# A fixed order for the opening loads and for VectorE's first steps in a two-layer mLSTM/Conformer trunk

## The chip, the core and the metric

The kernel runs on one core of one Trainium2 chip. The metric is the device time of one execution in microseconds (us); lower is better. Five engines matter: TensorE (PE; its weight loads are PEld), VectorE (DVE), ScalarE (ACT), GpSimd (POOL) and SyncE (SP), whose queue issues every transfer of this kernel.

## The reference, cut to what matters

Two layers work on x (512 tokens by 1024 features, float32). The opening of the first layer is what the change touches:

```python
c_act = silu(c)
mod = c_act @ w_ada[l] + b_ada[l]            # 1024 x 6144: six groups of 1024: shift, scale, gate, twice
sh_mix, sc_mix, gt_mix, sh_mlp, sc_mlp, gt_mlp = split(mod, 6)
h = rms_norm(x, g_pre_mix[l]) * (1 + sc_mix) + sh_mix
u = h @ w_in[l]                              # 1024 x 4096: mLSTM input, gate z, GLU a, GLU b
```

After it come the mLSTM heads, a causal convolution over 31 taps behind a GLU, an output projection, and a squared-ReLU MLP with 4096 hidden features. Each sub-layer is normalised, gated and added to x.

## The kernel before, in words

Features lie on partitions: x is eight tiles of 128 features by 512 tokens. A float32 product is made of three matmuls on rounded parts: weight-high by input-high, weight-high by input-low, weight-low by input-high (`passes`, lines 179 to 181). So every weight block is loaded as `raw`, rounded to its high part on ScalarE (L171), and the remainder is taken as the low part (L172); every input tile `hp[i]` has a high part (ScalarE, L359) and a low part (VectorE, L360).

The opening of layer 0 runs in this chain:

- x is loaded, squared on ScalarE (L811) and summed over tiles on VectorE (L813). TensorE sums over partitions (L816), VectorE scales (L817), GpSimd takes the power -1/2 (L818), and TensorE spreads the result over partitions into the bank `bc0` (L824).
- The vector c, broadcast as `cbc` and as the column `cc`, goes through silu (L212, L215, L216).
- Shift and scale of feature tiles 0 to 3 come from `ada_col` on VectorE: one multiply-and-sum over a transposed 128x1024 block (`wadt`, L274, 1.28 us each) per column, two columns per tile, and one small addition (L278).
- Shift and scale of tiles 4 and 5, and of 6 and 7, come from `ada_rows(2)` and `ada_rows(3)` on TensorE: four blocks `wadn` each, eight matmuls (L247), a copy on ScalarE (L250), four small matmuls (L252), three small VectorE steps (L260, L258).
- `make_h` forms tile i: s = x times scale times bc0 (VectorE, L353), then L359 and L360.
- Six banks collect the first six blocks of the input projection at once: per tile 18 matmuls (six blocks, three passes) with the block `win0[i]` (128x768). Then the projections of the mixer follow, beginning with `ps_mm<-slot,yt`; and the 31-tap convolution starts on VectorE (L429, L431), in 480 steps of 0.75 us over both layers, mostly beside TensorE's projections.

The program's order on each engine is set by a scheduler that simulates the program while it is built; `high_priority` shifts an instruction's claim, and `behind(later, earlier)` forces an order. Before the change the scheduler is free to choose the order of the loads and of most of VectorE's steps. Buffers: `raw` has four, `adr` (the blocks of `ada_rows(3)` and later) three, `slot` 25; each of SP's transfers takes one of eight semaphores in turn, so that a transfer is issued only when the eighth before it has landed.

Of the kernel before, what the change touches and what calls it, by code (L numbers as in the profile page):

```python
# [53 lines left out]
def trunk(ctx, tc, xT, vecs, bg, cst, ccol, crow, wadn, wadt, win, win0, wqkv, wgate, wout, wff1, wff2, yT):  # L54
# [34 lines left out]
    def slot(shape=(P, 2, T), dt=F32):  # L89
        return slots.tile(list(shape), dt, name="slot", tag="slot", bufs=NSLOT)  # L90
# [23 lines left out]
    def r32(ap):  # L114
        return ap.bitcast(F32R)
# [4 lines left out]
    cbc = slots.tile([P, 2, T], F32, name="cbc", tag="slot", bufs=NSLOT).rearrange("p a b -> p (a b)")  # L120
    x = [keep.tile([P, T], F32, name=f"x{i}") for i in range(NF)]
    cc = keep.tile([P, NF], F32, name="cc")
    sp.dma_start(out=cbc, in_=crow.broadcast_to([P, D]))
    sp.dma_start(out=cc, in_=ccol)
    for i in range(NF):
        sp.dma_start(out=x[i], in_=xT[i])
        if i == 4:
            sp.dma_start(out=cs, in_=cst)
    sp.dma_start(out=vv, in_=vecs)

    ident = cs[:, C_ID:C_ID + P]
    mask = cs[:, C_MASK:C_MASK + P]
# [27 lines left out]
    def wblock(src, alloc=None, lo_eng=None, pri=None):  # L160
        n = src.shape[-1]
        with tc.high_priority(offset=WPRI if pri is None else pri):
            flat = lambda t: t.rearrange("p a b -> p (a b)")
            raw = wpool.tile([P, n], F32, name="raw", tag="raw", bufs=RAW)
            if alloc is not None:
                hi, lo = flat(alloc())[:, 0:n], flat(alloc())[:, 0:n]
            else:
                hi = wpool.tile([P, n], F32, name="whi", tag="whi", bufs=WHI)
                lo = wpool.tile([P, n], F32, name="wlo", tag="wlo", bufs=WLO)
            sp.dma_start(out=raw, in_=src)  # L170
            act.copy(out=r32(hi), in_=raw)  # L171
            wlast[0] = (lo_eng or pool).tensor_tensor(r32(lo), raw, hi, op=ALU.subtract)  # L172
        return hi, lo
# [60 lines left out]
    def ada_rows(nb, tag, alloc=None):  # L234
# [3 lines left out]
        for kk in range(NF // 2):  # L238
            if alloc is not None:
                raw = alloc().rearrange("p a b -> p (a b)")  # L240
            else:
                raw = wpool.tile([P, D], F32, name="adr", tag="adr", bufs=ADR)
            sp.dma_start(out=raw, in_=wadn[nb, kk])
            for j in range(2):
                k = 2 * kk + j
                g = k % 4
                pe.matmul(bk[32 * g:32 * g + 32, :], cc[:, k:k + 1].broadcast_to([P, 32]), raw[:, j * T:(j + 1) * T],  # L247
                          start=(k < 4), stop=(k >= 4), skip_group_check=True)
# [15 lines left out]
    def ada_col(l, c, alloc=None):  # L264
# [4 lines left out]
            raw = alloc().rearrange("p a b -> p (a b)")  # L269
        else:  # L270
            raw = wpool.tile([P, D], F32, name="adr", tag="adr", bufs=ADR)
        sp.dma_start(out=raw, in_=wadt[l, c])
        m, ini = mods[l][:, c:c + 1], inits[l][:, c:c + 1]
        red = dve.tensor_tensor_reduce(raw, raw, cbc, scale, 0.0 if one else ini, ALU.mult, ALU.add, m)  # L274
        if last[0] is not None:
# [1 line left out]
        if one and alloc is not None:  # L277
            dve.tensor_tensor(m, m, ini, op=ALU.add)  # L278
        elif one:
            late.append((l, c))  # L280

    def ada_bias():

# [133 lines left out]
    def mixer(l, hp, pre):  # L417
# [167 lines left out]
                dve.tensor_tensor(gsb, gsb, acc, op=ALU.add)  # L585

        gw = keep.tile([P, 24, 32], F32, name="gw", tag="gw", bufs=1)
        sp.dma_start(out=gw, in_=wgate[l])

        def gates():  # L590
            pi = bank("mm")
# [231 lines left out]
    for c in range(NC):  # L823
        pe.matmul(bc0[:, c * P:(c + 1) * P], r0[:, c:c + 1].broadcast_to([P, P]), ident, start=True, stop=True)  # L824
    hp, pre = [], {}
    for j in range(NF // 2):
        if j > 1:
            ada_rows(j, "ax", slot if j == 2 else None)
        for i in (2 * j, 2 * j + 1):
            if j < 2:  # L830
                ada_col(0, i, slot)
                ada_col(0, 8 + i, slot)
            pre[i] = wblock(win0[i], slot, dve, 0)
            hp.append(slot())
            lasth = make_h(0, i, x[i], bc0, slice(0, T), hp[i], 8, 0)
            behind(lasth, wlast[0])
    sp.dma_start(out=bgt, in_=bg)
    for l in range(L):
        for o, name, f in ((0, "g_cn", 0.5), (8, "b_cn", 0.5), (16, "b_dw", 2.0)):
            behind(dve.tensor_scalar(hgb[:, l, o:o + 8], vec(name, l), f, None, op0=ALU.mult), lasth)  # L840
# [65 lines left out]
```

## Time and profile before

| | |
|---|---|
| runs shown | 1609.22, 1612.67, 1613.26 us; median 1612.67 |
| the profiled execution | 1609.4 us, of which its span is 1607.6 |
| TensorE busy | 1540.3 us (96% of the span), 8020 matmuls |
| VectorE, ScalarE, GpSimd busy | 878.1, 689.8, 799.8 us |
| chain that ended last | TensorE 79% of the span, VectorE 5%, ScalarE and GpSimd 2% each |

The profiled execution lies 1.8 us above its span, and 3.3 us below the median of the runs. Busy time is an average over the whole span; the change lies in the first 75 us.

### The profile page before, as it was taken

The numbers are of one execution on the slowest core, as the hardware profiler recorded it, in microseconds if no ns is written. First come the engines' busy times: TensorE is split into PE (matmuls) and PEld (weight loads), VectorE is DVE, ScalarE is ACT, GpSimd is POOL, SyncE is SP. The second block draws the span as 40 slices with busy tenths as digits, with TensorE's granted clock in tenths as the row PEclk, the third lists the DMA queues.
The fourth block names the chain that finished last, engine by engine and source line by source line (L and its number), as shares of the span: only waits on it lengthen the run. The fifth ranks groups of instructions, "written<-read, shape, count | busy, mean of one in ns | idle before, by whom it ended". The sixth has DMA issues, their size and how long they took to land.

```text
span 1607.6 us, 21227 instructions
## 1 busy us (share of the span) xinstructions
PE 1540.3 (96%) x8020; PEld 1258.6 (78%) x8020; DVE 878.1 (55%) x1761; ACT 689.8 (43%) x1168; POOL 799.8 (50%) x488
## 2 busy tenths in 40 slices
PE   4899998999999999999999999999999999999997
PEld 3676766678998888888899777676799988888887
DVE  6499999752253522347656999997326320012114
ACT  3254663453554322332452666445355432233243
POOL 0176662255744444445871877334674444444462
PEclk9999999999999999999999999999999999999999
DMA  8414333313413555566630222220241233322341
GB/s 327 176 53 140 133 124 106 135 48 105 131 54 111 195 197 178 184 196 233 226 105 8 78 74 79 92 66 27 89 138 62 80 94 101 94 92 92 96 128 53
DMA packets 56270, 188.91 MB, mean 118 GB/s; under 512 B 6376, under 2 KB 8552, under 8 KB 56168
## 3 DMA queue, kind: packets, MB, share of 16 engines
q1 hardware_dynamic: 56168, 187.56, 35.4%
q8 instruction: 63, 1.03, 0.3%
q14 instruction: 39, 0.32, 0.1%
HBM read 185.44 MB, written 2.10 MB: 117 GB/s over the span
## 4 chain that ended last, share of the span: by engine, by line
PE 79%; DVE 5%; ACT 2%; POOL 2%; issue 1%; DMA 0%; ACTq 0%; POOLq 0%; DVEq 0%
PE ps_mm L179 24%; PE ps_mm L180 24%; PE ps_mm L181 24%; PE ps_mm L662 2%; DVE ps_cv L431 2%; PE ps_mm L674 2%; PE ps_ax L318 1%; POOL wlo L172 1%; PE ps_ax L247 1%; ACT whi L171 1%; PE ps_ax L580 1%; PE ps_ax L344 0%; PE ps_ax L649 0%; POOL slot L156 0%; PE ps_ax L703 0%
## 5 line engine op out<-in xcount | busy, mean ns | idle before, releaser
L172 POOL TENSOR_TENSOR wlo<-raw,whi 128x1024 fp32r<-128x1024 f32 (+1 forms) x216 | 499.6, 2314 | 564.5 <-ACT whi L171 555.0
L179 PE MATMUL ps_mm<-slot,whi 128*128 128x512 f32 (+1 forms) x1632 | 623.6, 383 | 6.4 <-ACT slot L155 3.5
L181 PE MATMUL ps_mm<-slot,wlo 128*128 128x512 f32 (+1 forms) x1632 | 621.1, 381 | 5.3 <-POOL wlo L172 4.8
L180 PE MATMUL ps_mm<-slot,whi 128*128 128x512 f32 (+1 forms) x1632 | 622.3, 381 | 0.7 <-POOL slot L156 0.6
L171 ACT CAST whi<-raw 128x1024 fp32r<-128x1024 f32 (+1 forms) x216 | 216.7, 1003 | 497.2 <-PE ps_mm L180 362.8
L179 PEld LDWEIGHTS ps_mm<-slot,whi 128*128 128x128 f32 x1632 | 307.7, 189 | 76.4 <-issue 5.0
L181 PEld LDWEIGHTS ps_mm<-slot,wlo 128*128 128x128 f32 x1632 | 307.9, 189 | 73.6 <-POOL wlo L172 6.3
L180 PEld LDWEIGHTS ps_mm<-slot,whi 128*128 128x128 f32 x1632 | 308.0, 189 | 67.5 <-issue 4.7
L431 DVE SCALAR_TENSOR_TENSOR ps_cv<-slot,vv,ps_cv 128x512 f32<-128x512 f32 x480 | 333.3, 751 | 1.5
L769 DVE TENSOR_TENSOR ps_mm<-rl,ps_mm 128x512 f32<-128x512 f32 (+1 forms) x78 | 46.8, 600 | 284.6 <-ACT rl L768 284.5
L179 PE MATMUL ps_mm<-slot 128*128 128x256 f32 (+1 forms) x568 | 159.9, 295 | 17.9 <-ACT slot L359 11.0
L180 PE MATMUL ps_mm<-slot 128*128 128x256 f32 (+1 forms) x568 | 164.2, 292 | 0.1
L181 PE MATMUL ps_mm<-slot 128*128 128x256 f32 (+1 forms) x568 | 163.0, 290 | 0.0
L179 PEld LDWEIGHTS ps_mm<-slot 128*128 128x128 f32 x568 | 106.9, 193 | 22.7 <-ACT slot L359 13.7
L180 PEld LDWEIGHTS ps_mm<-slot 128*128 128x128 f32 x568 | 109.4, 193 | 2.7 <-issue 0.8
L181 PEld LDWEIGHTS ps_mm<-slot 128*128 128x128 f32 x568 | 109.3, 193 | 1.3
L172 POOL TENSOR_TENSOR slot<-raw,slot 128x1024 fp32r<-128x1024 f32 x34 | 85.2, 2524 | 14.4 <-issue 12.8
L274 DVE CUSTOM_DVE_ANT_0 adr<-adr,cbc,ini 128x1024 f32<-128x1024 f32 x40 | 66.4, 1671 | 23.3 <-DMA adr<-in_wadt 23.3
L147 POOL TENSOR_TENSOR small<-small,mhalf 128x4 f32<-128x4 f32 (+1 forms) x38 | 34.6, 910 | 84.6 <-DVE small L146 79.8
L771 DVE TENSOR_TENSOR slot<-ps_mm,slot 128x512 fp32r<-128x512 f32 (+1 forms) x78 | 46.4, 595 | 37.3 <-ACT slot L770 37.1
L532 POOL TENSOR_TENSOR xa<-xa,s 128x512 f32<-128x512 f32 x48 | 62.0, 1291 | 4.8 <-ACT s L531 1.6
L770 ACT CAST slot<-ps_mm 128x512 fp32r<-128x512 f32 (+1 forms) x78 | 39.9, 511 | 45.8 <-DVE ps_mm L769 45.8
(200 smaller groups left out, 1571.3 us busy)
## 6 DMA issues: line engine op xcount, KB each, us to landing
raw<-in_wff SPq DMA_DIRECT2D x138, 512.0 KB, 3.5
raw<-in_win SPq DMA_DIRECT2D x58, 512.0 KB, 3.3
adr<-in_wadt SPq DMA_DIRECT2D x56, 512.0 KB, 4.5
raw<-in_wout SPq DMA_DIRECT2D x36, 512.0 KB, 3.5
adr<-in_wadn SPq DMA_DIRECT2D x28, 512.0 KB, 4.4
raw<-in_wqkv SPq DMA_DIRECT2D x24, 256.0 KB, 2.6
slot<-in_wadt SPq DMA_DIRECT2D x8, 512.0 KB, 6.0
raw<-in_win SPq DMA_DIRECT2D x8, 384.0 KB, 7.4
```

Of the source, the lines that this page charges most:

```text
L147: pool.tensor_tensor(y, u, mhalf[:, 0:n], op=ALU.pow)
L171: act.copy(out=r32(hi), in_=raw)
L172: wlast[0] = (lo_eng or pool).tensor_tensor(r32(lo), raw, hi, op=ALU.subtract)
L179: pe.matmul(out, whi, xh, start=first, stop=False)
L180: pe.matmul(out, whi, xl, start=False, stop=False)
L181: mark[0] = pe.matmul(out, wlo, xh, start=False, stop=last)
L274: red = dve.tensor_tensor_reduce(raw, raw, cbc, scale, 0.0 if one else ini, ALU.mult, ALU.add, m)
L431: dve.scalar_tensor_tensor(acc, at[i][:, k:k + T], w, acc, op0=ALU.mult, op1=ALU.add)
L532: pool.tensor_tensor(acc, acc, tk, op=ALU.add)
L769: dve.tensor_tensor(o, rl[:, ts], o, op=ALU.mult)
L770: act.copy(out=r32(pr[:, 0, ts]), in_=o)
L771: last[0] = dve.tensor_tensor(r32(pr[:, 1, ts]), o, pr[:, 0, ts], op=ALU.subtract)
```

## The change

All loads of the opening go through `load`, and each is forced behind the one before it; all VectorE steps of the first tiles go through `step`, likewise. The loop over tiles is written out in that order: x first, then `cbc`, `vv`, `cc`; per tile the two `wadt` blocks around `win0`; `ada_rows(2)` stands after tile 1 and `ada_rows(3)` after tile 3 (before: after tile 3 and after tile 5 in the program text); for tiles 0 to 2 the next tile's `ada_col` steps stand around this tile's low parts. The loads of `gw` (gate weights) and `bgt` are put behind the opening's last load.

```diff
     for i in range(NF):
-        sp.dma_start(out=x[i], in_=xT[i])
-        if i == 4:
-            sp.dma_start(out=cs, in_=cst)
-    sp.dma_start(out=vv, in_=vecs)
+        load(x[i], xT[i])
+        if i == 3:
+            load(cs, cst)
+    load(cbc, crow.broadcast_to([P, D]))
+    load(vv, vecs)
+    load(cc, ccol)
...
-        sp.dma_start(out=gw, in_=wgate[l])
+        g = sp.dma_start(out=gw, in_=wgate[l])
+        if l == 0:
+            behind(g, queue[0])
...
-    for j in range(NF // 2):
-        if j > 1:
-            ada_rows(j, "ax", slot if j == 2 else None)
-        for i in (2 * j, 2 * j + 1):
-            if j < 2:
-                ada_col(0, i, slot)
-                ada_col(0, 8 + i, slot)
-            pre[i] = wblock(win0[i], slot, dve, 0)
-            hp.append(slot())
-            lasth = make_h(0, i, x[i], bc0, slice(0, T), hp[i], 8, 0)
-            behind(lasth, wlast[0])
-    sp.dma_start(out=bgt, in_=bg)
+    SPLIT = 4
+    step(laststat)
+    for c in (0, 8):
+        step(ada_col(0, c, slot))
+    for i in range(NF):
...
+        load(raw, win0[i])
+        act.copy(out=r32(hi), in_=raw)
+        pre[i] = hi, lo
+        pr, t, sh = slot(), s2(), mods[0][:, i:i + 1]
+        hp.append(pr)
+        step(dve.scalar_tensor_tensor(t, x[i], mods[0][:, 8 + i:9 + i], bc0, op0=ALU.mult, op1=ALU.mult))
+        act.activation(out=r32(pr[:, 0, :]), in_=t, func=AF.Identity, bias=sh)
+        if i + 1 < SPLIT:
+            step(ada_col(0, i + 1, slot))
+            lasth = step(dve.scalar_tensor_tensor(r32(pr[:, 1, :]), t, sh, pr[:, 0, :], op0=ALU.add, op1=ALU.subtract))
+            step(dve.tensor_tensor(r32(lo), raw, hi, op=ALU.subtract))
+            step(ada_col(0, 9 + i, slot))
+        else:
+            step(dve.tensor_tensor(r32(lo), raw, hi, op=ALU.subtract))
+            lasth = step(dve.scalar_tensor_tensor(r32(pr[:, 1, :]), t, sh, pr[:, 0, :], op0=ALU.add, op1=ALU.subtract))
+        if i in (1, 3):
+            ada_rows(2 + i // 2, "ax", slot if i == 1 else None)
+    behind(sp.dma_start(out=bgt, in_=bg), queue[0])
+    ordered[0] = False
```

Three places where instructions moved. First SP's queue right after x, `cs`, `cbc`, `cc` and `vv`. Here `in_wadt` feeds `ada_col`, `in_wadn` feeds `ada_rows`, and `in_win0` is a tile's weight block. Before:

```order
L272 DMA slot_156<-in_wadt 128x1024
L272 DMA slot_159<-in_wadt 128x1024
L243 DMA adr_277<-in_wadn 128x1024
L243 DMA adr_281<-in_wadn 128x1024
L243 DMA adr_285<-in_wadn 128x1024
L837 DMA bgt_75<-in_bg 4x4
L588 DMA gw_338<-in_wgate 128x768
L170 DMA raw_163<-in_win0 128x768
L170 DMA raw_181<-in_win0 128x768
L170 DMA raw_199<-in_win0 128x768
L170 DMA raw_217<-in_win0 128x768
L272 DMA slot_174<-in_wadt 128x1024
```

After, from the same place:

```order
L127 DMA slot_156<-in_wadt 128x1024
L127 DMA slot_159<-in_wadt 128x1024
L127 DMA raw_165<-in_win0 128x768
L127 DMA slot_172<-in_wadt 128x1024
L127 DMA slot_177<-in_wadt 128x1024
L127 DMA raw_183<-in_win0 128x768
L127 DMA slot_190<-in_wadt 128x1024
L127 DMA slot_195<-in_wadt 128x1024
L127 DMA slot_200<-in_wadn 128x1024
L127 DMA slot_204<-in_wadn 128x1024
L127 DMA slot_208<-in_wadn 128x1024
L127 DMA slot_212<-in_wadn 128x1024
```

Three blocks of `ada_rows(3)` and `gw` have left the place ahead of the first `win0`, and the four blocks of `ada_rows(2)` have come up to before the third. A little later in SP's queue after the change:

```order
L127 DMA raw_245<-in_win0 128x768
L127 DMA adr_255<-in_wadn 128x1024
L127 DMA adr_259<-in_wadn 128x1024
L127 DMA adr_263<-in_wadn 128x1024
L127 DMA adr_267<-in_wadn 128x1024
L127 DMA raw_282<-in_win0 128x768
L127 DMA raw_293<-in_win0 128x768
L127 DMA raw_304<-in_win0 128x768
L127 DMA raw_315<-in_win0 128x768
L871 DMA bgt_75<-in_bg 4x4
L607 DMA gw_338<-in_wgate 128x768
L127 DMA adr_880<-in_wadn 128x1024
```

The four last blocks `win0` now stand behind the fourth block of `ada_rows(3)`, which needs a buffer of the three `adr` and so waits for TensorE's matmuls on the first.

Second, VectorE's queue at tiles 0 and 1 (`cbc` marks `ada_col`, `s2` is the product s, the `slot` with `raw` a weight's low part). Before:

```order
L353 SCALAR_TENSOR_TENSOR s2_170<-x0_77,mod0_101,ps_ax_151 128x512
L172 TENSOR_TENSOR slot_165<-raw_163,slot_164 128x768
L360 SCALAR_TENSOR_TENSOR slot_169<-s2_170,mod0_101,slot_169 128x512
L172 TENSOR_TENSOR slot_183<-raw_181,slot_182 128x768
L274 ISA slot_174,mod0_101<-slot_174,cbc_76,ini0_103 128x1024
L274 ISA mod0_101 128x1
L274 ISA slot_177,mod0_101<-slot_177,cbc_76,vv_74 128x1024
L274 ISA mod0_101 128x1
L278 TENSOR_TENSOR mod0_101<-mod0_101,ini0_103 128x1
L353 SCALAR_TENSOR_TENSOR s2_188<-x1_78,mod0_101,ps_ax_151 128x512
L360 SCALAR_TENSOR_TENSOR slot_187<-s2_188,mod0_101,slot_187 128x512
L172 TENSOR_TENSOR slot_201<-raw_199,slot_200 128x768
```

After:

```order
L859 SCALAR_TENSOR_TENSOR s2_169<-x0_77,mod0_101,ps_ax_151 128x512
L292 ISA slot_172,mod0_101<-slot_172,cbc_76,ini0_103 128x1024
L292 ISA mod0_101 128x1
L863 SCALAR_TENSOR_TENSOR slot_168<-s2_169,mod0_101,slot_168 128x512
L864 TENSOR_TENSOR slot_164<-raw_165,slot_163 128x768
L292 ISA slot_177,mod0_101<-slot_177,cbc_76,vv_74 128x1024
L292 ISA mod0_101 128x1
L296 TENSOR_TENSOR mod0_101<-mod0_101,ini0_103 128x1
L859 SCALAR_TENSOR_TENSOR s2_187<-x1_78,mod0_101,ps_ax_151 128x512
L292 ISA slot_190,mod0_101<-slot_190,cbc_76,ini0_103 128x1024
L292 ISA mod0_101 128x1
L863 SCALAR_TENSOR_TENSOR slot_186<-s2_187,mod0_101,slot_186 128x512
```

One `ada_col` of the next tile has come between a tile's product s and its low part, and the weight's low part now belongs to the tile itself, not to the next one.

Third, TensorE's queue around `ada_rows(2)` (`ps_ax<-slot,cc` are its matmuls). Before it stands behind tile 3:

```order
L181 MATMUL ps_cx<-slot 128x512
L247 MATMUL ps_ax<-slot,cc 32x512 x8
L252 MATMUL ps_ax<-cs,s_245 128x1 x4
L247 MATMUL ps_ax<-adr,cc 32x512 x6
L179 MATMUL ps_mm<-slot 128x512 x3
```

After it stands behind tile 1, and the matmuls of `ada_rows(3)` (`ps_ax<-adr,cc`) follow in two pairs around tile 3's first pass and four behind tile 3:

```order
L199 MATMUL ps_cx<-slot 128x512
L265 MATMUL ps_ax<-slot,cc 32x512 x8
L270 MATMUL ps_ax<-cs,s_216 128x1 x4
L197 MATMUL ps_mm<-slot 128x512 x3
L197 MATMUL ps_cv<-slot 128x512 x2
```

The two `ada_rows` no longer stand together ahead of tile 4. From the end of tile 7 on, every engine's queue holds the same instructions as before with local exchanges of neighbours; the largest are some of the convolution's transposes on TensorE, 13 to 52 matmuls earlier among the projections of layer 0.

## Rows read from the trace of the kernel before

**Rows 1.** Busy time by stretch: stretch in us, its length, then busy us (and instructions) of PE, PEld, DVE, ACT and POOL, the granted clock of TensorE, the busy share of the DMA engines (over 1 is full), GB/s.

```profile
0.00:21.66 21.66, 3.94 (x16) 3.56 (x17) 10.65 (x23) 10.15 (x16) 2.29 (x6) 1.00 0.93 354
21.66:75.30 53.64, 44.61 (x193) 32.02 (x194) 30.28 (x58) 15.67 (x22) 7.39 (x8) 0.97 0.64 234
```

**Rows 2.** Waits of TensorE before 75.3 us: who waited for whom, us in total, times, longest.

```profile
PE ps_mm L179 <- ACT slot L359: 10.5, 6, 2.6
```

**Rows 3.** Transfers of the opening. A line that begins with a time is an issue on SP's queue (start us, us of issuing); the line under it is that transfer alone: KB, and us from issue to landing. The last line but one is from the page: a smaller weight load, median over the span. The last line is the traffic from 8 to 27 us.

```profile
1.65 0.42 SPq L126 DMA_DIRECT2D x<-in_xT  x1
x<-in_xT SPq DMA_DIRECT2D x1, 256.0 KB, 3.6
...
5.43 0.45 SPq L126 DMA_DIRECT2D x<-in_xT  x1
x<-in_xT SPq DMA_DIRECT2D x1, 256.0 KB, 5.3
...
11.75 0.33 SPq L170 DMA_DIRECT2D raw<-in_win  x1
raw<-in_win SPq DMA_DIRECT2D x1, 384.0 KB, 8.4
...
raw<-in_wqkv SPq DMA_DIRECT2D x24, 256.0 KB, 2.6
...
DMA packets 2620, 7.73 MB, mean 407 GB/s; under 512 B 299, under 2 KB 307, under 8 KB 2620
```

**Rows 4.** Timeline of the chain to the first tile: start us, us, engine, line, operation, and in brackets the idle time before and what ended it.

```profile
9.43 2.03 ACT L811 ACTIVATE s<-x 128x512 f32<-128x512 f32 x3 [0.80 <-DMA x<-in_xT]
12.43 1.87 PE L816 MATMUL ps_ax<-cs,rl 128*128 128x1 f32 x8 [12.43 <-DVE rl L813]
13.54 1.23 DVE L216 SCALAR_TENSOR_TENSOR cbc<-raw,cbc 128x1024 f32<-128x1024 f32 x1 [0.70 <-ACT cbc L215]
14.68 0.15 DVE L817 TENSOR_SCALAR small<-ps_ax 128x4 f32<-128x4 f32 x1
...
17.02 2.08 PE L824 MATMUL ps_ax<-cs,small 128*128 128x128 f32 x8 [2.72 <-POOL small L818]
...
19.13 0.75 DVE L353 SCALAR_TENSOR_TENSOR s<-x,mod,ps_ax 128x512 f32<-128x512 f32 x1 [1.65 <-DMA gw<-in_wgate]
20.15 0.83 ACT L171 CAST slot<-raw 128x768 fp32r<-128x768 f32 x1 [6.31 <-DMA raw<-in_win]
20.89 0.72 ACT L359 ACTIVATE slot<-s,mod 128x512 fp32r<-128x512 f32 x1
```

**Rows 5.** Timeline of VectorE at tile 1.

```profile
24.36 1.28 DVE L274 CUSTOM_DVE_ANT_0 slot<-slot,cbc,ini 128x1024 f32<-128x1024 f32 x1 [0.86 <-DMA slot<-in_wadt]
...
28.69 0.75 DVE L360 SCALAR_TENSOR_TENSOR slot<-s,mod,slot 128x512 fp32r<-128x512 f32 x1 [0.79 <-ACT slot L359]
...
29.42 0.96 DVE L172 TENSOR_TENSOR slot<-raw,slot 128x768 fp32r<-128x768 f32 x1
```

**Rows 6.** Timeline of TensorE: first matmuls of tile 0, its last one, first matmuls of tiles 1, 2, 3, 4, 6 and 7, and the first matmul after the opening.

```profile
21.66 1.65 PE L179 MATMUL ps_mm<-slot 128*128 128x512 f32 x3 [2.57 <-ACT slot L359]
...
27.09 0.39 PE L181 MATMUL ps_cx<-slot 128*128 128x512 f32 x1
28.71 0.97 PE L179 MATMUL ps_mm<-slot 128*128 128x512 f32 x3 [1.23 <-ACT slot L359]
...
34.57 0.96 PE L179 MATMUL ps_mm<-slot 128*128 128x512 f32 x3 [1.42 <-ACT slot L359]
...
40.43 0.96 PE L179 MATMUL ps_mm<-slot 128*128 128x512 f32 x3 [1.39 <-ACT slot L359]
...
52.56 0.97 PE L179 MATMUL ps_mm<-slot 128*128 128x512 f32 x3 [1.74 <-ACT slot L359]
...
65.27 1.34 PE L179 MATMUL ps_mm<-slot 128*128 128x512 f32 x3 [2.12 <-ACT slot L359]
...
71.10 0.85 PE L179 MATMUL ps_mm<-slot 128*128 128x512 f32 x3
...
75.28 0.39 PE L179 MATMUL ps_mm<-slot,yt 128*128 128x512 f32 x1
```

**Rows 7.** Timeline of `ada_rows(2)` on TensorE and ScalarE; the fourth pair of matmuls of `ada_rows(3)`; and the load of that pair's block, alone on the queue (KB, us from issue to landing).

```profile
44.80 1.92 PE L247 MATMUL ps_ax<-slot,cc 128*32 128x512 f32 x16
46.79 0.59 ACT L250 COPY s<-ps_ax 128x512 f32<-128x512 f32 x1 [5.68 <-PE ps_ax L247]
47.42 1.05 PE L252 MATMUL ps_ax<-cs,s 128*128 128x1 f32 x8 [0.70 <-ACT s L250]
...
57.41 1.05 PE L247 MATMUL ps_ax<-adr,cc 128*32 128x512 f32 x4
...
adr<-in_wadn SPq DMA_DIRECT2D x1, 512.0 KB, 3.3
```

**Rows 8.** Busy time by stretch as in rows 1: from the last matmul of tile 5 to tile 6, and tile 6's first ten matmuls.

```profile
62.20:65.20 3.00, 0.95 (x9) 0.86 (x7) 1.79 (x5) 0.71 (x2) 0.71 (x6) 1.00 0.77 266
65.27:69.00 3.73, 3.73 (x10) 2.92 (x11) 3.23 (x15) 1.30 (x2) 0.00 (x0) 0.55 0.33 83
```

**Rows 9.** Timeline at one of the convolution's transposes in layer 0: VectorE's last step for it, and TensorE's transposes that read it.

```profile
182.01 1.36 DVE L492 TENSOR_SCALAR csb<-ps_cx,small 128x128 f32<-128x128 f32 x4
...
186.84 0.60 PE L496 MATMUL ps_cx<-cs,csb 128*128 128x128 f32 x4
```

More of the change, by code (lines that the diff above doesn't have):

```diff
@@ L122, in trunk, with load, step @@
     cc = keep.tile([P, NF], F32, name="cc")
-    sp.dma_start(out=cbc, in_=crow.broadcast_to([P, D]))
-    sp.dma_start(out=cc, in_=ccol)
-    for i in range(NF):
-        sp.dma_start(out=x[i], in_=xT[i])
-        if i == 4:
-            sp.dma_start(out=cs, in_=cst)
-    sp.dma_start(out=vv, in_=vecs)
+    queue, steps, ordered = [None], [None], [True]
+    def load(out, in_):
+        d = sp.dma_start(out=out, in_=in_)
+        if ordered[0]:
+            if queue[0] is not None:
+                behind(d, queue[0])
+            queue[0] = d
+        return d
+    def step(inst):
+        if ordered[0]:
+            if steps[0] is not None:
+                behind(inst, steps[0])
+            steps[0] = inst
+        return inst
+    for i in range(NF):
+        load(x[i], xT[i])
[4 more added lines that the diff above has]
+    load(cc, ccol)
     ident = cs[:, C_ID:C_ID + P]
@@ L169, in wblock @@
                 lo = wpool.tile([P, n], F32, name="wlo", tag="wlo", bufs=WLO)
-            sp.dma_start(out=raw, in_=src)
+            load(raw, src)
             act.copy(out=r32(hi), in_=raw)
@@ L242, in ada_rows @@
                 raw = wpool.tile([P, D], F32, name="adr", tag="adr", bufs=ADR)
-            sp.dma_start(out=raw, in_=wadn[nb, kk])
+            load(raw, wadn[nb, kk])
             for j in range(2):
@@ L271, in ada_col @@
             raw = wpool.tile([P, D], F32, name="adr", tag="adr", bufs=ADR)
-        sp.dma_start(out=raw, in_=wadt[l, c])
+        load(raw, wadt[l, c])
         m, ini = mods[l][:, c:c + 1], inits[l][:, c:c + 1]
@@ L280, in ada_col @@
             late.append((l, c))
+        return red
     def ada_bias():
@@ L825, in trunk @@
     hp, pre = [], {}
-    for j in range(NF // 2):
-        if j > 1:
-            ada_rows(j, "ax", slot if j == 2 else None)
-        for i in (2 * j, 2 * j + 1):
-            if j < 2:
-                ada_col(0, i, slot)
-                ada_col(0, 8 + i, slot)
-            pre[i] = wblock(win0[i], slot, dve, 0)
-            hp.append(slot())
-            lasth = make_h(0, i, x[i], bc0, slice(0, T), hp[i], 8, 0)
-            behind(lasth, wlast[0])
-    sp.dma_start(out=bgt, in_=bg)
+    SPLIT = 4
[3 more added lines that the diff above has]
+    for i in range(NF):
+        hi, lo = slot().rearrange("p a b -> p (a b)")[:, 0:6 * P], slot().rearrange("p a b -> p (a b)")[:, 0:6 * P]
+        raw = wpool.tile([P, 6 * P], F32, name="raw", tag="raw", bufs=RAW)
+        load(raw, win0[i])
[17 more added lines that the diff above has]
+    ordered[0] = False
     for l in range(L):
```

## The prediction

> **What bounds the kernel now.** The overview says TensorE is busy for 96% of the span and leads the chain that ended last for 79% of it. So I looked for the stretches where TensorE does not work, with the table by stretch first [rows 1]: it is busy for 3.9 of the first 21.66 us, and 44.6 of the next 53.64, and the end of a matmul is modelled, so busy is not work done. The waits [rows 2] then say what it waits for: ScalarE's high part of an input tile (L359), 10.5 us in six waits. To see what those 53.6 us hold, I read the first matmul of each tile [rows 6]. Tile 7 runs without a gap: 71.10 to 75.28, 4.18 us for its 18 matmuls. At that price seven tiles cost 29.26 us; tile 0, with its slow first matmuls, costs 5.66 (21.66 to 27.09, and 0.23 for the last). Together 34.92 us, so 18.7 us of the stretch are something else: 1.39 before tile 1, 1.68 before each of tiles 2 and 3, 7.95 between tiles 3 and 4 (`ada_rows`), 4.35 between the starts of tiles 4 and 6 beyond two tiles' work, and 1.65 in tile 6 at a slower clock.
>
> The start itself is a chain of single steps [rows 4]: ScalarE squares x as it lands, VectorE sums, TensorE sums over partitions (12.43), VectorE scales (14.68, late because the silu step of `cbc` at 13.54 stands ahead of it and ends at 14.77), GpSimd, TensorE (17.02 to 19.10), VectorE's product s (19.13). Then ScalarE sits in L171 until 20.15, because the first `win0` has only just landed: issued at 11.75, 8.4 us to landing [rows 3]. L359 is queued behind that L171, and TensorE behind L359. All transfers share one pipe, full at 407 GB/s from 8 to 27 us [rows 3], so 512 KB cost 1.29 us of it, 384 KB 0.97.
>
> After 75.28 us nothing is tied to a point in time: weights are loaded and split ahead, and VectorE's convolution starts from the opening's results as TensorE's projections do. What the opening loses or saves goes to the end one to one, unless the local exchanges behind it cost something.
>
> **The change, step by step.**
>
> *x to the head of the queue.* x's first tile was issued at 1.65 behind `cbc` and `cc`; now it takes the place at 0.74 that `cbc` had, 0.91 earlier, and 512 KB (1.3 us of pipe) leave its way. First to last tile took 5.48 us (landings 5.25 and 10.73) [rows 3], and that is kept. The first tile's own latency is not shown for an empty queue: at least 2.6 us, the profile's median for 256 KB transfers later, at most the 3.6 of the row [rows 3]. So x7 lands between 8.8 and 9.8; I take 9.1, nearer the lower end, since nothing is ahead. Squares then end 0.7 later, at 9.8 instead of 11.46: 1.7 us earlier (bounds 1.0 to 2.0). L817 no longer stands behind the silu step: another 0.35. So TensorE's bank `bc0` is done at 17.05 instead of 19.10. The other branch keeps up: `cbc` lands 1.3 behind x7 at 10.4, two ScalarE steps of about 1 end at 12.5, and on VectorE, from 12.85 behind L817, the silu step (1.23) and two `ada_col` (1.28 each) with small steps [rows 4, 5] come to some 4: 16.85.
>
> *First `win0` behind two `wadt` blocks.* From x7's landing 2.4 MB of loads lead to it, 5.9 us: landed at 15.0, cast before s is there. L359 follows s at once: s 17.1 to 17.85, high part 17.9 to 18.6, and TensorE starts at 18.65 instead of 21.66 [rows 4, 6]. **Start: -3.0 us.**
>
> *VectorE's order at tiles 0 to 2.* Per tile it has two `ada_col` steps of 1.28, s 0.75, the weight's low part 0.96 and the input's 0.75 [rows 4, 5]: 5.0 us, above the 4.18 of a tile on TensorE, and that costs the gaps of 1.39 and 1.68. Now one `ada_col` fits into ScalarE's time for L359. Stepping through: tile 0's low parts are there at 20.8, s of tile 1 at 23.1, its high part at 23.9. TensorE leaves tile 0 at 18.65 + 5.66 = 24.3. So the 1.39 before tile 1 is gone, and tile 1 ends at 28.5, its low parts (24.85, 25.8) being in time.
>
> *`ada_rows(2)` ahead of tile 2.* Its four blocks are some 7.0 MB behind x7: landed at 26.2, before TensorE is there. Eight matmuls 2.0 us, copy 0.6, four matmuls 1.05 [rows 7]: 28.6 to 32.25. ScalarE has the copy, a weight cast and L359 in a row, so tile 2 can begin at 32.7. VectorE waits for this too: its three small steps stand ahead of the next `ada_col` and of tile 2's low part, which comes at 34.95, 0.85 after TensorE has done the first six matmuls. Tile 2 ends at 37.75: 4.2 and 0.85 us lost.
>
> *`ada_rows(3)` around tile 3.* A pair of its matmuls costs 1.0 with what lies around it (57.41 to 58.39) [rows 7]. First pair to 38.8; tile 3's high part at 38.95 (VectorE did `ada_col`, the addition and s from 35.75 to 38.2); six matmuls, second pair, twelve matmuls: 44.15. Lost: 1.25 and 1.0. Then four matmuls, the copy (45.9), L359, tile 4 at 47.0: 2.85 lost. SP is held meanwhile: the fourth `adr` block is issued only when the first pair is done, 38.9, and four `win0`, `gw` and the next loads are queued behind it. At 3.3 us alone [rows 7] it is there at 42.2, 2 us before TensorE asks; the next `win0` lands at some 43.3 and is cast by 44.2, 1.1 us before the copy behind it on ScalarE. So I cost this at nothing, with a cover of 1 to 2 us.
>
> *Tiles 4 to 7* have no `ada_col`: VectorE needs 2.5 us per tile, TensorE 4.18. 47.0 + 4 x 4.18 = 63.7 for the first matmul after the opening, against 75.28. Lost in all 10.15 instead of 18.7: **-8.55 us**. The weights of the projection that follows are issued by 52, cast after tile 7's L359 (some 53 us) and split on GpSimd by 59: in time for 63.7.
>
> **Sum.** -3.0 - 8.55 = -11.55: 1609.4 - 11.5 = 1597.9 for the profiled execution. It lies 3.3 below the median of the runs shown and 1.7 below the mean of those three and itself (1611.1); by that mean I forecast **1600 us**.
>
> *The clock, a rule weighed.* In tile 6 the granted clock is 0.55 (the 1.2 GHz level), after 3 us with only 0.95 busy; after the 1.74 us of waiting before tile 4 it was not lowered [rows 6, 8]. The lowered stretch cost 1.65 us. The Trainium skill's page "TensorE: Matmul & The Clock Gate", section "HAM oscillation — how this bites in real kernels", says that TensorE's clock is halved again whenever it waits too long between groups of matmuls, and that every such wait costs anew. The trace agrees for tile 6. By that rule both `ada_rows` would be followed by a slow stretch, since now each is a pause of its own; by the rows of tile 4, neither. The sum above goes by the rows; the rule is the second rival.
>
> **The rivals.**
>
> 1. *The held queue.* The cover of the fourth `adr` block and the `win0` behind it is 1 to 2 us by my sum, whose steps each may be 0.3 off. If the `win0` comes 3 us later than I say, tile 4 starts 2 us later: -9.5, 1601.5 us. For it: nothing else can be issued while SP waits. Against: the pipe is empty by then.
> 2. *A lowered clock after each `ada_rows`*: two stretches at 1.65 us each, none before: -8.2, 1603 us. For it: TensorE has only four tiny matmuls for about 2.1 us before tile 2, and 1.7 before tile 4. Against: tile 4 before, as said.
> 3. *The transposes of the convolution in layer 0*, some 13 to 52 matmuls (3 to 12 us) earlier among the projections. TensorE works in order: a transpose that stands ahead of VectorE's result holds all projections behind it. The slack was 3.5 us at one of them (183.4 to 186.8 [rows 9]); moved by 26 matmuls, 6 us, it could wait 2.5. Four moved ones together are moved by some 26 us. If VectorE's results also shift less than TensorE's work, this eats 3 to 9 of the gain: 1603 to 1609, no change from some 6.8 on. It decides against the change when more than 11.5 + 4.8 = 16.3 of those 26 us are waited for, which gives over 1616 us: slower. Against: VectorE's convolution is moved up with the opening, and the slack was left in most places.
> 4. *No such gain, because something later absorbs it*: a wait on a transfer would. The pipe is far from full after the opening, so I give it little: within 4.8, 1611 us.
>
> **How the numbers follow.** 0.3% is 4.8 us, about what a measurement of this kernel can tell from no change. Chances: the forecast 0.58 (its own range 1596 to 1603: start bounds -1.0 to +0.7, steps 0.3 each, the level of the runs 1.7 either way); rival 1 0.10; rival 2 0.10; rival 3 eating some of the gain 0.13, of which 0.06 still faster by over 4.8; rival 3 turned slower 0.04; rival 4 0.05. Faster 0.58 + 0.10 + 0.10 + 0.06 = 0.84; slower 0.04; within 0.3% 0.12. The range for 8 in 10 goes from 1595, the forecast with every bound on the good side, to 1607, which takes in rivals 1 and 2 and half of 3.
>
> **What would show it.** Right: the first matmul of tile 0 near 18.7, no gap before tile 1, the first matmul after the opening (`ps_mm<-slot,yt`) near 63.7, the same matmul count from there to the end in the same 1532 us. Wrong start: x's squares end near 11 instead of 9.8, or ScalarE still waits for `win0`. Wrong middle: TensorE waits for a block of `ada_rows(3)`, or ScalarE for a `win0` (L855 after the change), before tile 4; or the granted clock near tile 2 or 4 is about half. Wrong end: waits of TensorE on the transposes (L500, L515 after the change) between 110 and 310 us where there were hardly any.

## The result, and the profile after

The changed kernel takes 1596.85 us in the median of four executions (1595.56 to 1600.35); the one before, with a fourth execution beside the three shown, 1612.31. The ratio is 0.9911, 95% interval 0.9889 to 0.9933: faster by 15.5 us, where 0.3% is 4.8. The forecast was 1600, from 1595 to 1607.

The profiled execution of the changed kernel took 1600.35 us, with a span of 1598.6 and a mean granted clock of 0.986 (before 1607.6 and 0.990). So the two traces differ by 9 us, the medians by 15.5; that gap comes up again below. Of the twelve executions of one run below (only the order of VectorE's steps) one took 2551 us, at a mean granted clock of 0.557, and the numbers given there leave it out.

Busy time by stretch, columns as in [rows 1]: up to the first matmul of tile 0, and from there to the first matmul behind the opening.

```profile
0.00:19.78 19.78, 3.94 (x16) 3.56 (x16) 10.93 (x23) 10.34 (x16) 2.17 (x6) 1.00 0.90 338
19.78:67.36 47.58, 45.66 (x193) 32.44 (x194) 29.76 (x59) 16.14 (x22) 7.41 (x8) 0.96 0.75 280
```

The same 193 matmuls that took 53.64 us now take 47.58, and they begin 1.88 earlier: the opening ends at 67.36 instead of 75.28, **7.92 us earlier where 11.55 was forecast**. TensorE's waits in it, all there are:

```profile
PE ps_ax L837 <- DVE rl L834: 12.0, 1, 12.0
PE ps_ax L845 <- POOL small L839: 2.3, 1, 2.3
PE ps_mm L197 <- ACT slot L860: 1.9, 2, 1.6
PE ps_ax L270 <- ACT s L268: 1.5, 2, 0.8
```

The six waits on ScalarE's high part, 10.5 us [rows 2], have become two of 1.9 (L860 is the old L359). The start, as the timelines of ScalarE, TensorE and VectorE have it:

```profile
8.18 2.71 ACT L832 ACTIVATE s<-x 128x512 f32<-128x512 f32 x4 [0.58 <-DMA x<-in_xT]
11.98 1.87 PE L837 MATMUL ps_ax<-cs,rl 128*128 128x1 f32 x8 [11.98 <-DVE rl L834]
13.88 0.16 DVE L838 TENSOR_SCALAR small<-ps_ax 128x4 f32<-128x4 f32 x1 [0.67 <-PE ps_ax L837]
16.11 2.07 PE L845 MATMUL ps_ax<-cs,small 128*128 128x128 f32 x8 [2.27 <-POOL small L839]
16.25 0.83 ACT L855 CAST slot<-raw 128x768 fp32r<-128x768 f32 x1 [2.29 <-DMA raw<-in_win]
18.23 0.75 DVE L859 SCALAR_TENSOR_TENSOR s<-x,mod,ps_ax 128x512 f32<-128x512 f32 x1 [0.32 <-DMA slot<-in_wadt]
19.01 0.72 ACT L860 ACTIVATE slot<-s,mod 128x512 fp32r<-128x512 f32 x1 [1.93 <-DVE s L859]
```

The squares end at 10.89 (before 11.46 [rows 4]), the weight's cast (L855) is over before s begins, and L838 follows L837 at once. Then TensorE: tile 0's first matmul and its last, tile 1's first and last, `ada_rows(2)`, tile 2, the pairs of `ada_rows(3)` around tile 3, tile 4, tile 5's first, and the first matmul behind the opening (compare [rows 6, 7]).

```profile
19.78 0.79 PE L197 MATMUL ps_mm<-slot 128*128 128x512 f32 x1 [1.59 <-ACT slot L860]
26.62 0.40 PE L199 MATMUL ps_cx<-slot 128*128 128x512 f32 x1
26.86 0.62 PE L197 MATMUL ps_mm<-slot 128*128 128x512 f32 x2
30.77 0.39 PE L199 MATMUL ps_cx<-slot 128*128 128x512 f32 x1
31.09 1.92 PE L265 MATMUL ps_ax<-slot,cc 128*32 128x512 f32 x16
33.75 1.05 PE L270 MATMUL ps_ax<-cs,s 128*128 128x1 f32 x8 [0.73 <-ACT s L268]
35.10 0.51 PE L197 MATMUL ps_mm<-slot 128*128 128x512 f32 x1 [0.30 <-ACT slot L860]
41.29 1.05 PE L265 MATMUL ps_ax<-adr,cc 128*32 128x512 f32 x4
42.27 0.96 PE L197 MATMUL ps_mm<-slot 128*128 128x512 f32 x3
47.81 1.06 PE L265 MATMUL ps_ax<-adr,cc 128*32 128x512 f32 x8
50.58 0.71 PE L197 MATMUL ps_mm<-slot 128*128 128x512 f32 x2
54.81 0.39 PE L197 MATMUL ps_mm<-slot 128*128 128x512 f32 x1
67.36 0.39 PE L197 MATMUL ps_mm<-slot,yt 128*128 128x512 f32 x1
```

Tile 0 takes 7.08 us to tile 1's first matmul, tile 1 4.23, tile 2 6.19, tiles 4 to 7 together 16.78. Tile 2's stretch has the granted clock at 0.72, a mean over stretches at the 2.4 and the 1.2 GHz level; in tile 4's it is 1.00:

```profile
35.10:41.29 6.19, 6.09 (x19) 4.12 (x19) 6.08 (x12) 1.40 (x2) 0.00 (x0) 0.72 0.02 4
50.58:54.81 4.23, 4.23 (x20) 3.46 (x20) 4.23 (x9) 2.47 (x5) 0.00 (x0) 1.00 1.02 414
```

Between `ada_rows(3)`'s last matmuls and tile 4, ScalarE shows what the held queue cost: its cast of the next `win0` begins at 46.72 when that block has landed, and then ScalarE waits 1.47 us for TensorE.

```profile
46.72 0.84 ACT L855 CAST slot<-raw 128x768 fp32r<-128x768 f32 x1 [5.71 <-DMA raw<-in_win]
49.03 0.59 ACT L268 COPY s<-ps_ax 128x512 f32<-128x512 f32 x1 [1.47 <-PE ps_ax L265]
```

### The profile page after: what moved, and what is told of

The parts are those of the page before. It is cut to its first block, busy times and chain, and to the rows that moved or that the text cites. A ratio compares the mean times of both kernels' runs of the same rounds, so it can differ in the third digit from the quotient of the medians.

```text
span 1598.6 us, 21226 instructions
## 1 busy us (share of the span) xinstructions
PE 1541.6 (96%) x8020; PEld 1258.7 (79%) x8020; DVE 876.3 (55%) x1761; ACT 690.3 (43%) x1168; POOL 799.3 (50%) x488
## 4 chain that ended last, share of the span: by engine, by line
PE 78%; DVE 3%; ACT 2%; POOL 1%; issue 0%; DMA 0%; POOLq 0%; ACTq 0%
PE ps_mm L197 23%; PE ps_mm L199 23%; PE ps_mm L198 23%; PE ps_mm L695 2%; PE ps_mm L683 2%; PE ps_ax L337 1%; POOL wlo L190 1%; ACT whi L189 1%; PE ps_ax L265 1%; PE ps_ax L670 0%; PE ps_ax L599 0%; PE ps_ax L363 0%; DVE ps_cv L450 0%; PE ps_ax L724 0%; PE ps_cx L500 0%
## 5 line engine op out<-in xcount | busy, mean ns | idle before, releaser
L198 PE MATMUL ps_mm<-slot 128*128 128x256 f32 (+1 forms) x568 | 163.3, 292 | 0.2
L190 POOL TENSOR_TENSOR slot<-raw,slot 128x1024 fp32r<-128x1024 f32 x34 | 86.4, 2563 | 12.8 <-issue 11.2
```

The costliest lines, as they stand in the source:

```text
L198: pe.matmul(out, whi, xl, start=False, stop=False)
```

## The experiments

Twelve further runs were made, in three groups; each group was timed beside the kernel before on its chip (1610.35, 1611.09 and 1610.53 us in the median).

### Again: the changed kernel unaltered

> The changed kernel once more, unaltered. Its first trace has the first matmul after the opening at 67.4 us (75.3 before), 3.7 us later than forecast, and 1531.2 us from there to the end (1532.3 before): 9.0 us less span, while the medians of the runs differ by 15.5 us. Theory: the opening itself varies between executions (x's landings, and how long TensorE stays at its lower clock in tiles 0 and 2), so this trace ends the opening somewhere between 63.7 and 67.4 us with the same 1531 us behind it. Rival: the opening ends at 67.4 us again, and it is the 1531 us behind it that vary by several us from run to run, so that part of the 15.5 us is chance.

Measured: 1595.05 us (1593.28 to 1600.79), ratio 0.9911, interval 0.9894 to 0.9928. Its trace has tile 0 at 19.75 and the end of the opening at 66.81. Both the gain and the shape of the opening repeat. Behind the opening this trace has 1532.2 us, so it does not decide between the theory and its rival.

### Only the new order of the transfers

```diff
     def step(inst):
-        if ordered[0]:
-            if steps[0] is not None:
-                behind(inst, steps[0])
-            steps[0] = inst
         return inst
```

> The changed kernel without the fixed order of VectorE's steps; the loads keep theirs. VectorE now does both low parts of a tile before the next tile's first ada_col. Theory: TensorE then waits again before tiles 1 and 2, about 1 us each, as before the change (1.39 and 1.68 us), so the opening ends some 2 to 3 us later than with the change, about 70 us; time about 2.5 us above the changed kernel. Rival (the order of VectorE's steps is worth nothing, the loads do it all): the opening ends within 1 us of the changed kernel's.

Measured: 1599.94 us (1595.17 to 1602.48), ratio 0.9929, interval 0.9911 to 0.9946; the opening ends at 68.34. VectorE, left to the scheduler, makes a tile's low parts and then the next two `ada_col` steps, and TensorE waits no more for that than in the changed kernel: the end of the opening is 1.0 us later, as the rival says. The time, though, lies 4.9 us above that of the changed kernel beside it (1595.05; 2.8 us by the mean spans), more than the opening shows, and where the rest is lost is not known. Of the whole gain some 10 us come with the transfers and with where `ada_rows` stands.

### Only the order of VectorE's steps

```diff
     def load(out, in_):
         d = sp.dma_start(out=out, in_=in_)
         if ordered[0]:
-            if queue[0] is not None:
-                behind(d, queue[0])
             queue[0] = d
         return d
```

> The changed kernel without the forced order of the loads beyond the first twelve; VectorE's steps keep theirs. Three blocks of ada_rows(3) and then four win0 stand ahead of tile 1's ada_col blocks. Theory: 1.5 MB more ahead of the first win0 makes it land 3.9 us later, so TensorE starts tile 0 near 21.7 us instead of 19.8, and tile 1's ada_col blocks land near 25 us, so tile 1 starts near 28.7 instead of 26.9; the opening ends 3 to 5 us later than with the change. Rival (VectorE's order is what matters): within 1 us of the changed kernel.

Measured: 1606.66 us (1604.8 to 1610.72), ratio 0.998, interval 0.997 to 0.999: 3.7 us of gain. The opening ends at 71.94, 4.6 us later than in the changed kernel, as the theory says; tile 1 begins at 30.79, later than its 28.7. The time lies 11.6 us above the changed kernel's, and for the 7 us of it that are not in the opening no cause is shown. Without its order SP issues three `adr` blocks and four `win0` ahead of tile 1's `wadt`, and VectorE's fixed order, in which tile 0's low part stands behind the next `ada_col`, hangs on that `wadt`. The timeline of TensorE shows where: tile 0 at 21.44, then a wait on the input's low part (L861) inside tile 0 and another inside tile 1.

```profile
21.44 1.65 PE L195 MATMUL ps_mm<-slot 128*128 128x512 f32 x3 [3.52 <-ACT slot L858]
26.12 1.65 PE L196 MATMUL ps_mm<-slot 128*128 128x512 f32 x3 [1.75 <-DVE slot L861]
34.17 0.98 PE L196 MATMUL ps_mm<-slot 128*128 128x512 f32 x3 [1.82 <-DVE slot L861]
```

Here the fixed order on VectorE is worth no more than the order of its inputs lets it be.

### Only x at the head of the queue, in the kernel before

```diff
-    sp.dma_start(out=cbc, in_=crow.broadcast_to([P, D]))
-    sp.dma_start(out=cc, in_=ccol)
...
     for i in range(NF):
-        sp.dma_start(out=x[i], in_=xT[i])
-        if i == 4:
-            sp.dma_start(out=cs, in_=cst)
-    sp.dma_start(out=vv, in_=vecs)
+        load(x[i], xT[i])
+        if i == 3:
+            load(cs, cst)
+    load(cbc, crow.broadcast_to([P, D]))
+    load(vv, vecs)
+    load(cc, ccol)
```

> The kernel before with only the first twelve loads in the new order: x and cs, then cbc, vv, cc. Theory: the first win0 has the same bytes ahead of it as before and still lands near 20 us, and tile 0's high part is queued behind its cast, so TensorE starts tile 0 at 21 to 21.7 us and nothing else moves: time 0 to 1 us below the kernel before. Rival (x at the head is the gain): tile 0 starts 2 us earlier, time 2 us below.

Measured: 1611.15 us (1607.79 to 1615.36), ratio 1.0001, interval 0.999 to 1.0012: nothing. The timeline of TensorE: start, tile 0, and the first matmul behind the opening:

```profile
12.07 1.87 PE L824 MATMUL ps_ax<-cs,rl 128*128 128x1 f32 x8 [12.07 <-DVE rl L821]
16.21 2.07 PE L832 MATMUL ps_ax<-cs,small 128*128 128x128 f32 x8 [2.27 <-POOL small L826]
22.49 1.65 PE L187 MATMUL ps_mm<-slot 128*128 128x512 f32 x3 [4.21 <-ACT slot L367]
...
77.36 0.39 PE L187 MATMUL ps_mm<-slot,yt 128*128 128x512 f32 x1
```

The statistics are as early as in the changed kernel (16.21 against 16.11), and the 0.8 us won there are lost with interest in front of tile 0, in 4.21 us of waiting for ScalarE, 1.6 more than before [rows 6]: ScalarE casts the first `win0` at 20.98, where it did at 20.15 [rows 4]. So tile 0 starts 0.8 us later than before (expected was no later than 21.7), and in this trace the opening ends 2.1 us later; the time does not show them. Moving x forward alone did not pay here; in the changed kernel, where the first `win0` and its two `wadt` come forward with it, tile 0 starts at 19.78.

### `ada_rows(2)` and `(3)` back behind tiles 3 and 5

```diff
-        if i in (1, 3):
-            ada_rows(2 + i // 2, "ax", slot if i == 1 else None)
+        if i in (3, 5):
+            ada_rows(1 + i // 2, "ax", slot if i == 3 else None)
```

> The changed kernel with ada_rows(2) and ada_rows(3) moved back to behind tiles 3 and 5, where they stood before, all else as changed. Theory: each ada_rows costs TensorE about the same pause wherever it stands, and what the change gained is the start and the gaps before tiles 1 to 3: the first matmul behind the opening at 66 to 70 us, the time within 3 us of the changed kernel's. Rival: the gain of the middle is that the pauses were moved to where ScalarE and VectorE need the time anyway: the opening is 5 us or more longer, 72 us or later, and the time 5 us or more longer than the changed kernel's.

Measured: 1604.81 us (1602.6 to 1609.66), ratio 0.9963, interval 0.9951 to 0.9975; the opening ends at 71.00. That is 9 us above the changed kernel's 1595 to 1597 on other chips, 3.6 to 4.2 of them in the opening; for the others, behind it, no cause is shown. The rival holds in the sum (5 us or more), though its 72 us at the end of the opening was 1 too many: a pause of `ada_rows` is cheaper behind tiles 1 and 3. The last pair then has its pause before tile 6, with the lowered clock that stood there before as well (0.66 from 60 to 65 us).

### Where the gain lies: both kernels cut off behind the opening, and behind the mixer

```diff
         at[0], at[1], at[2] = glu_start(3)
+        do_xm(0)
+        ada_rows(4, "ax")
+        (write those tiles as the output)
+        return
```

> The kernel before, cut off behind the opening: it ends after the eight tiles, the first two sixteenths' projections of the mixer and the first ada_rows behind them, and writes tiles made there as the output. Everything later of both layers is left out, so its time stands only beside that of opening_after, the same cut of the changed kernel. Two theories of where the 15 to 16 us between the medians of the full kernels lie, of which the two traces show 7.9 us in the opening (75.28 against 67.36 us at the first matmul behind it) and 1 us behind it. A: the traces show the opening as it is in every execution, and the rest of the gain lies behind it: the two cuts differ by 7 to 9 us. B: the profiled executions of the changed kernel lost clock in the opening that other executions did not lose, and nearly the whole gain is made there: the cuts differ by 11 to 15 us. Between 9 and 11 it stays open.

> The changed kernel, cut off at the same place as opening_before (everything behind the opening and the first two projections is left out). A: 7 to 9 us less than opening_before. B: 11 to 15 us less. In its trace the first matmul of tile 0 is expected at 19.8 and the first matmul behind the tiles at 66.8 to 67.4, as in the two traces of the full kernel.

Measured: 94.03 us (91.22 to 96.89) and 86.24 us (84.31 to 86.67): 7.8 us, theory A; the shortest of each differ by 6.9. But these cuts are not the opening of the full kernels. From tile 6 on TensorE's queue is another: the matmuls of the next `ada_rows` stand among the last tiles, in the cut of the kernel before in the pause ahead of tile 6, and tile 6 then runs at full pace (66.71 to 70.92, 4.21 us). In the second cut the first matmul behind the tiles comes at 69.61, not at 66.8 to 67.4. So the cuts speak against B, but they do not show that other executions of the full kernels have the opening of the traces. In five of the six executions of the second the mean clock was near 0.972, in one 0.990, and that one is the shortest, 84.31: this fits a lowered clock at tile 2 in most of them.

```diff
         hp, pre = mixer(l, hp, pre)
-        hp, pre = mlp(l, hp, pre)
+        for i in range(NF):
+            sp.dma_start(out=yT[i], in_=hp[i][:, 0, :])
+        break
```

> The kernel before, cut off behind the mixer of layer 0: it ends when the input tiles of that layer's MLP are made, and writes these as the output. The MLP of layer 0 and all of layer 1 are left out, so its time stands only beside that of mixer_after, the same cut of the changed kernel. The cuts behind the opening differ by 7.8 us, the full kernels by 15 to 16 us between their medians; where does the rest lie? A: in the convolution of layer 0, which begins from the opening's results and whose steps stand in another order now: the two cuts differ by 12 to 15 us. B: behind the mixer, or nowhere in particular (stretches of lowered clock that fall differently on the two kernels): the cuts differ by 6 to 9 us. The traces of the full kernels show 5.8 us at this place, the profiled execution of the changed kernel having lost 6 us more of clock up to there.

> The changed kernel, cut off at the same place as mixer_before (the MLP of layer 0 and all of layer 1 are left out). A: 12 to 15 us less than mixer_before. B: 6 to 9 us less.

Measured: 487.51 us (484.63 to 490.05) and 476.32 us (475.20 to 477.25): 11.2 us, between the two expectations. Here TensorE's queue is that of the full kernels up to the cut. The first matmul behind the opening, in the first cut's trace and in the second's:

```profile
77.81 0.39 PE L179 MATMUL ps_mm<-slot,yt 128*128 128x512 f32 x1
```

```profile
65.88 0.39 PE L197 MATMUL ps_mm<-slot,yt 128*128 128x512 f32 x1
```

They are 11.9 us apart, of 13.8 between the spans of the two traces (488.3 and 474.5). In the first, the matmuls of `ada_rows(3)` ahead of tile 4 ran at a clock of 0.53, 3.52 us for the 1.91 that they took in the full kernel's trace. So the end of the opening varies between executions, 75.28 and 77.81 us before the change and 65.88 to 67.72 after it, and the gain in it is 7.6 to 11.9 us, depending on which traces are set side by side. How the 15 us divide between the opening and the rest is open.

### Work for TensorE ahead of tile 0

```diff
+    junk = bank("mm")
+    spin = [lastv]                # the last matmul of the sum over partitions
...
+    def warm(n):
+        for _ in range(n):
+            m = pe.matmul(junk[:, 0:P], ident, ident, start=True, stop=True)
+            behind(m, spin[0])
+            spin[0] = m
+
+    warm(4)
     for c in range(NC):
-        pe.matmul(bc0[:, c * P:(c + 1) * P], r0[:, c:c + 1].broadcast_to([P, P]), ident, start=True, stop=True)
+        m = pe.matmul(bc0[:, c * P:(c + 1) * P], r0[:, c:c + 1].broadcast_to([P, P]), ident, start=True, stop=True)
+        behind(m, spin[0])
+        spin[0] = m
+    warm(3)
```

> The changed kernel with seven more matmuls on TensorE before tile 0, on data that nobody reads: four of 128 columns ahead of the four that make bc0 (L845) and three behind them. Tile 0 took 7.08 us in the changed kernel, 5.66 in the one before and 4.18 would be a tile at full clock. Theory: tile 0 is slow because TensorE comes to it after a stretch with almost nothing to do, and the clock is raised only after some work; with work ahead of it tile 0 takes 5.7 us or less, the first matmul behind the opening comes at 65.4 to 66 instead of 66.8 to 67.4, and the time falls by about 1.4 us. Rival: the slow tile 0 comes of its inputs (low parts late), so the matmuls change nothing: tile 0 7 us, same time within 0.5 us; or they delay bc0 by their own length, some 0.5 us slower.

Busy time of 20 to 25 us, first in the changed kernel, then with the seven matmuls; and tile 0's, tile 2's first matmul and the end of the opening in the latter:

```profile
20.00:25.00 5.00, 5.00 (x12) 3.90 (x13) 4.93 (x9) 1.30 (x2) 0.00 (x0) 1.00 1.03 415
```

```profile
20.00:25.00 5.00, 4.55 (x20) 3.37 (x19) 4.93 (x9) 1.15 (x2) 0.00 (x0) 1.00 1.03 417
...
19.54 0.97 PE L197 MATMUL ps_mm<-slot 128*128 128x512 f32 x3 [0.41 <-ACT slot L873]
24.46 0.95 PE L197 MATMUL ps_mm<-slot 128*128 128x512 f32 x3 [0.45 <-ACT slot L873]
32.79 0.96 PE L197 MATMUL ps_mm<-slot 128*128 128x512 f32 x3 [0.30 <-ACT slot L873]
64.00 0.39 PE L197 MATMUL ps_mm<-slot,yt 128*128 128x512 f32 x1
```

Tile 0 now takes 4.92 us instead of 7.08, with 20 matmuls in those 5 us for 12: the theory holds, by more than it said. The clock column reads 1.00 in both rows, but the records of the granted clock in the trace begin only at 25.92 us in the changed kernel and at 18.92 here, and the column counts the time ahead of them as 1.00. In the changed kernel the matmuls of 512 columns go from one per 0.43 us to one per 0.23 at that record; with the seven it comes before tile 0. Tile 2 keeps its clock too (it took 6.19), and the opening ends at 64.00, 3.4 us earlier. The time was 1593.89 us (1592.15 to 1601.16), ratio 0.9901, interval 0.9885 to 0.9917, on another chip than the changed kernel's. So both ran once more, on one:

> The changed kernel once more, unaltered, on one chip with warm_2: a second sample of its time and a third trace. Expected 1594 to 1597 us; if its profiled execution is one of clock 0.988 or more, the part from the first matmul behind the opening to the end should take 1527 to 1529 us, as in warm, against 1532 before: then the gain behind the opening is real and the two traces so far hid it by clock.

> The kernel warm once more, on one chip with after_2. In its first run the opening was 3.4 us shorter than in the changed kernel's traces (64.00 against 67.36 us), 1.4 expected; the median was 1593.9 us on another chip. Theory: those 3.4 us are kept to the end: 1591 to 1593 us, 3 us or more under after_2. Rival: the stages behind take most of them back, since VectorE sets the end of the convolution: 0 to 1.5 us under after_2.

Measured: 1595.94 us (1593.55 to 1599.99) for the changed kernel, 1597.99 (1595.78 to 1601.29) for the one with seven matmuls, whose opening ended at 63.6 in its trace. The opening is shorter in both of its traces, and the time is not: over all of them 12 executions of the one have the same mean as 16 of the other (spans 1594.9 and 1594.8 us). The rival holds in its effect, but not by its mechanism: the traces carry the 3 to 4 us through to the end (spans 1591.6 and 1594.0 against 1598.6, 1599.0 and 1596.2). Where the executions that leave no trace give them back is not known. As a faster version it is not shown.

The third trace of the changed kernel, with a clock of 0.987, took 1528.5 us behind the opening (67.7 to 1596.2), as long as was expected for a clock a little higher, and 3.8 less than the trace of before.

## Why the prediction was right, and where it was not

The median lies in the range, 3 us under the forecast, and in part that is luck. In the traces of the two full kernels the opening gave 3.6 us less than forecast: the start cost 1.1 us more than the sum had, tile 0 1.4 and tile 2 1.2. The time fell by 4 us more than forecast all the same, and where that lies is not shown.

**The start: -3.0 forecast, -1.88 measured.** The step that failed is x's landing: "first to last tile took 5.48 us, and that is kept". The queue moved 309 GB/s between 2 and 8 us, against 339 before, though x was now at its head. From its first landing to its last it took 6.76 us (3.42 to 10.18); x's last transfers took 5.6 us from issue to landing where 5.3 [rows 3] was the pattern, and landed near 10.2 instead of 9.1. Everything behind was late by that 1.1 and by nothing else: s, high part and tile 0 followed at the distances that were forecast. The cast of `win0` and L838 went as said.

**Tile 0: 5.66 forecast, 7.08 measured.** The price was taken from before [rows 6] as if it belonged to the tile. It belongs to what TensorE did before it, as the runs with seven matmuls ahead show.

**No gap before tile 1**: right; tile 1 follows tile 0 without a wait, and the run in which VectorE kept its order but the transfers were free shows on what it rests: there TensorE waits inside tiles 0 and 1 for low parts that are queued behind a late `wadt`.

**`ada_rows(2)`**: the pause was forecast at 4.2 us and is 4.10 (31.00, 0.23 after tile 1's last matmul began, to 35.10). Behind it tile 2 took 6.19 us instead of the 5.03 said: the clock was lowered. That is half of the second rival, one stretch of its two. The Trainium skill ("TensorE: Matmul & The Clock Gate", section "HAM oscillation — how this bites in real kernels") says that a long enough wait between groups of matmuls halves TensorE's clock again, each time anew; the prediction took both pauses for such waits. Here the clock fell at tile 2, behind a pause in which TensorE ran 12 small matmuls and waited 0.73 us at the longest, and not at tile 4, behind 2.86 us with 8 such; and the runs with more work ahead of tile 0 kept it at tile 2 as well, with the same pause (28.78 to 32.79 in the first of them). The rule names the right suspect, but the pause alone does not decide.

**`ada_rows(3)`, tile 4 and the held queue**: right almost to the digit. 2.85 us were forecast before tile 4, 2.86 are there; the queue held behind the fourth `adr` block cost nothing, with 1.47 us to spare where a cover of 1 to 2 was forecast. Tiles 4 to 7 take 16.78 for 16.72.

**The rest, "the same 1532 us": open.** The first two traces bear it out (1532.3 and 1531.2), and so does the second of the changed kernel (1532.2); the third has 1528.5. But the medians differ by more than the openings of these traces do. Three things are shown. First, VectorE sets the pace from the opening to the gates:

```profile
75.28:238.30 163.02, 155.96 (x721) 112.05 (x719) 156.08 (x276) 90.73 (x147) 106.67 (x86) 0.99 0.32 108
```

```profile
67.36:230.70 163.34, 156.72 (x722) 113.19 (x721) 155.86 (x278) 90.27 (x147) 106.14 (x86) 0.97 0.32 110
```

The first row is before, the second after: VectorE (the third busy time) works 156 of 163 us in both, and in all ten full traces this stage takes 162.4 to 163.6. The granted clock, third from the end, is lower after the change (0.97 for 0.99, some 3 us of 163), and the stage takes as long: lost clock cost no time here. What the opening saves does reach the gates whole, as forecast. Second, TensorE's waits behind the gates, until layer 0's gates are transposed and put together (238.3 to 270.6 before, 230.7 to 266.7 after), first before, then after:

```profile
PE ps_ax L627 <- DVE s L614: 3.0, 1, 3.0
PE ps_mm L593 <- DVE gsb L585: 1.7, 1, 1.7
PE ps_mm L179 <- ACT s L446: 1.2, 1, 1.2
```

```profile
PE ps_cx L500 <- ACT csb L497: 2.2, 1, 2.2
PE ps_mm L197 <- ACT slot L566: 1.3, 1, 1.3
PE ps_mm L614 <- DVE gsb L604: 0.8, 1, 0.8
```

5.9 us have become 4.3. The third rival's mechanism is there (TensorE waits 2.2 us on a transpose, L500, where it waited for none), but it took the place of a wait of 3.0 for the gates: 1.6 us less waiting instead of a loss of 3 to 9. Yet in these two traces the stretch took longer after the change, 36.0 us for 32.3, with the clock lowered in it (0.90 for 1.00, worth some 3.5 us). That is not the change's doing alone: in the trace with only x moved forward, whose TensorE queue is that of before, the clock was lowered there too, and it took 35.2 us. The two rows:

```profile
238.30:270.60 32.30, 28.06 (x126) 19.26 (x127) 32.30 (x64) 11.21 (x14) 8.63 (x5) 1.00 0.38 127
```

```profile
230.70:266.70 36.00, 32.48 (x132) 20.44 (x132) 32.67 (x64) 12.74 (x17) 8.21 (x5) 0.90 0.32 114
```

Third, the profiled execution of the changed kernel was the longest or second longest in each of its three groups (1600.35, 1600.79, 1597.97), with more lowered clock: 1.4% of 1598.6 us against 1.0% of 1607.6, 6 us. Over all executions the two kernels have the same clock (0.988 and 0.987). So the 9 us between the two traces would be 6 short of the truth, and that would close the gap to the medians, if lost clock always cost time; but some 3 of these 6 us were lost between the opening and the gates, where they cost none. The rest of the gap may lie in the opening itself, which ended 11.9 us earlier in the traces of the kernels cut off behind the mixer, not 7.9. Neither is shown to be the cause.

Rival 4 (something later absorbs it) is refuted; rival 1 did not occur.

## What to carry to other kernels

An order of transfers and an order of steps are one change: x forward alone gave 0, VectorE's order without that of the transfers 4 us, the transfers' order with the new places of `ada_rows` 10, all together 15. Take the price of a tile together with what the engine did before it, since a "slow first tile" belongs to the idle time and not to the tile. And where the clock varies, set two traces against each other only after asking what each lost of it: here 9 us of 15.5 could be seen in the first two, another pair had 11.9 us in the opening alone, and where the rest lies stayed open.

## What the hardware showed that was not expected

- TensorE's first matmuls after a long idle start run at half the pace: one of 512 columns per 0.43 us up to the first record of the granted clock in the trace (25.92 us; 24.70 before the change), one per 0.23 from there on. The profile's column counts the time without a record as 1.00, so it does not show this: 12 matmuls in 5 us (20 to 25 us), 20 in the same 5 us after seven more matmuls ahead of them.
- x at the head of the queue did not arrive at the later rate: between 2 and 8 us the DMA engines were 0.93 busy and moved 309 GB/s with eight x tiles at the head, 339 before, 415 at 20 to 25 us.
- An opening shorter by 3.4 us, present in two traces, left no mark on the mean of 12 executions.
- Where VectorE sets the pace, a lower clock of TensorE cost nothing: 163.3 us at 0.97, 163.0 at 0.99.
